# The opening of a hybrid decoder block: the first norm's modulation on VectorE and TensorE instead of GpSimd

## The chip, the cores and the metric

The kernel runs on one core of a Trainium2 chip. The metric is the device time of one execution in microseconds, taken as the median of several runs. A core has five engines that run side by side and meet through semaphores: TensorE (PE in the profile), VectorE (DVE), ScalarE (ACT), GpSimd (POOL) and SyncE (SP), which issues all the transfers (DMAs) of this kernel. Each engine works through its own queue strictly in order.

## The reference

One block on 1024 tokens of width 1024 in float32. A conditioning vector `c` gives six vectors for shift, scale and gate; the first two modulate the first norm:

```python
mod = jax.nn.silu(c) @ w_ada[l] + b_ada[l]
sh1, sc1, g1, sh2, sc2, g2 = jnp.split(mod, 6, axis=-1)
h = modulate(rms_norm(x, norm1_g[l]), sh1, sc1)      # h * (1 + sc1) + sh1
x = x + g1[:, None, :] * token_mixer(h, w_in[l], ...)
h = modulate(rms_norm(x, norm2_g[l]), sh2, sc2)
x = x + g2[:, None, :] * squared_relu_mlp(h, w_ff1[l], w_ff2[l])
return rms_norm(x, norm_f_g)
```

`rms_norm` multiplies by `rsqrt(mean(x*x) + 1e-6)` of each token. The token mixer has a retention branch of four heads and a dilated attention branch of twelve, with a relative bias that is looked up from a table of 32 buckets; both start from `h @ w_in`.

## The kernel before, in words

Everything is kept transposed: a tile `xt[k]` holds 128 of the 1024 channels on its partitions and all 1024 tokens along the free axis (`k` = 0 to 7). A product of full precision is made of three: every operand is split into a high part (`hh`, `raw_..h`, rounded by ACT) and a low part (`hl`, `raw_..l`, the remainder, by DVE), and `mm3` issues low x high, high x low and high x high. A column block of a projection is thus 8 x 3 products for each half of the tokens.

The change touches the opening, which ends where the regular steps begin.

- `startup` loads `c`, the bias table, the eight `xt` tiles, constants (`ct`, `vec`), the first three weight tiles (`raw`) and the columns of `w_ada` for the scale and the shift of the first norm, sixteen tiles of 512 KB called `em` (`early_mod`, nine buffers). The order in which these loads are issued is written out by hand; SP's queue keeps it.
- `cb` is silu(c), spread over all partitions. One element of the scale or shift vector per partition is the sum over the free axis of `em * cb` (`mod1_mul`, `mod1_sum`). For the six tiles `i = SC1 + k` with `k` = 0, 1, 2, 4, 6 and the first shift tile, DVE does product and sum in one instruction (line 328). For the other ten GpSimd multiplies (line 330) and ACT sums (line 338).
- ACT squares the `xt` tiles, DVE adds them into `acc1`; `rstd_rows` sums over the partitions by eight products with a column of ones (in two chains, one for each half of the tokens), DVE scales, GpSimd raises to the power -0.5; `rstd_bcast` spreads the result over the partitions by products with the identity, and ACT copies it to `rb1`.
- `bias_row` looks up one row of the relative bias for each of twelve heads by a product that writes the same row to all 128 partitions; ACT copies it (`rows`), and at the end of the opening SP stores each of the twelve to DRAM (line 635), where the attention reads it much later.
- `h1_scale(k)` adds the bias of the shift (line 357), makes the factor (line 358), scales `xt[k]` by factor and `rb1` (line 361) and lets ACT add the shift and round it to `hh[k]` (line 362). `h1_low(k)` forms `hl[k]` on DVE (line 365).
- `step_first` runs three column blocks at once, `q0`, `q1` and `k0` (two halves `k0a`, `k0b`), tile by tile as `h` becomes ready; the blocks of the last tiles follow in one piece. Its queue order on each engine is the order of the calls in the loop. `step_third` rotates the results; then comes `qkp`, the second block of the keys, and `v`, with four tiles of `w_rv`.

Weight tiles come through a ring of three buffers (`Steps.run`): a tile is loaded when the one three before it has been split.

Of the kernel before, what the change touches and what calls it, by code (L numbers as in the profile page):

```python
# [10 lines left out]
F32 = mybir.dt.float32  # L11
# [116 lines left out]
def block_kernel(ctx, tc, io, stop=None, dbg=None):  # L128
# [3 lines left out]
    def fv(t):  # L132
        return t.bitcast(F32)
# [77 lines left out]
    spool = st_ctx.enter_context(tc.tile_pool(name="spool", bufs=1))  # L211
    xt = [spool.tile([P, S], F32, name=f"xt{k}") for k in range(NK)]
    rb1 = spool.tile([P, S], F32, name="rb1")
    bias_d = [[dram.tile([P, 384], F32, name=f"biasd{g}_{a}") for a in range(4)] for g in range(3)]
    early = []

    def early_mod():

        i = len(early)
        if i < 16:  # L220
            t = spool.tile([P, 1024], F32, tag="em", bufs=9, name=f"em{i}")
            nc.sync.dma_start(t, io["w_ada"][(SC1, SH1)[i % 2] + i // 2])
            early.append(t)

# [14 lines left out]
    def rstd_bcast(rs, b0, nb, name):  # L239
# [4 lines left out]
                             ident, start=True, stop=True)  # L244
        return rb[:, :nb * P]

    bs1 = spool.tile([P, NK], F32, name="bs1")
    rel = spool.tile([P, 12], F32, name="rel")
    onehot = spool.tile([P, 3 * 384], F32, name="onehot")
    rows = spool.tile([P, 12, 384], F32, name="rows")  # L250
    crow = spool.tile([P, S], F32, tag="sq", bufs=2, name="crow")[:1]
    orow = spool.tile([P, S], F32, tag="sq", bufs=2, name="orow")[:1, :P]
    acc1 = spool.tile([P, S], F32, name="acc1")
    first = {}

    def startup(issue, prepare, n_gate, n_loads):
        first["release"] = lambda: issue(n_gate)
        first["release all"] = lambda: issue(n_loads)
        nc.vector.memset(rel, 0.0)
        nc.vector.memset(rel[32:33], 1.0)  # L260
        nc.vector.memset(orow, 1.0)
        nc.gpsimd.memset(onehot, 0.0)
# [11 lines left out]
        issue(2)  # L274
        early_mod()
        early_mod()
        issue(3)
        for _ in range(5):
            early_mod()
        pc = ps_mm("pc")  # L280
        for j in range(2):
            nc.tensor.matmul(pc[:, j, :], orow, crow[:, j * 512:(j + 1) * 512], start=True, stop=True)
        nc.scalar.activation(cb, pc.rearrange("p a b -> p (a b)"), AF.Silu)
        for k in range(NK):
            for j in ((slice(0, S),) if k < NK - 1 else (slice(0, 512), slice(512, S))):
                if k == 0:
                    nc.scalar.activation(acc1, xt[k], AF.Square)
                else:
                    sq = spool.tile([P, S], F32, tag="sq", bufs=2, name=f"sq{k}")
                    nc.scalar.activation(sq[:, j], xt[k][:, j], AF.Square)  # L290
                    nc.vector.tensor_add(acc1[:, j], acc1[:, j], sq[:, j])
            copies, products = (((), ()), ((), ()), ((), (0, 1, 2)), ((0,), (3,)), ((1, 2), (4, 5)),
                                ((3, 4), (6, 7)), ((5, 6), (8,)), ((7, 8), (9,)))[k]
            for i in copies:
                bias_copy(i)
            for i in products:
                bias_row(i)
        rs = [rstd_rows(acc1[:, j * 512:(j + 1) * 512], f"n1{j}", spool) for j in range(2)]
        bias_copy(9)
        prepare(1)  # L300
        mod1(0)
        nc.vector.tensor_scalar_add(bs1, vec[:, VC_BADA + SC1:VC_BADA + SC1 + NK], 1.0)
        prepare(1)
        mod1_mul(1)
        for j in range(2):
            nc.scalar.copy(rb1[:, j * 512:(j + 1) * 512], rstd_bcast(rs[j], 0, 4, f"n1{j}"))
        for i in (10, 11):
            bias_row(i)
        h1_scale(0)
        first["low"]()  # L310
        h1_low(0)
        mod1_sum(1)

    def bias_row(i):

        first[i] = ps_s(f"pb{i}")
        nc.tensor.matmul(first[i][:, :384], rel[:, i:i + 1].to_broadcast([P, P]),
                         onehot[:, (i // 4) * 384:(i // 4 + 1) * 384], start=True, stop=True)

    def bias_copy(i):  # L320
        nc.scalar.copy(rows[:, i, :], first.pop(i)[:, :384])

    def mod1_mul(k):

        for i in (SC1 + k, SH1 + k) if k < NK else ():
            t = early[2 * k + (i < SC1)]
            if k == 0 or i >= SC1 and k not in (3, 5, 7):
                nc.vector.scalar_tensor_tensor(t, t, 1.0, cb, op0=ALU.mult, op1=ALU.mult, accum_out=mods[:, i:i + 1])
            else:
                nc.gpsimd.tensor_mul(t, t, cb)  # L330
                first["sum", k] = first.get(("sum", k), []) + [(t, i)]

    def mod1_sum(k, n=2):

        while n > 0 and first.get(("sum", k)):
            n -= 1
            t, i = first["sum", k].pop(0)
            nc.scalar.activation(t, t, AF.Identity, accum_out=mods[:, i:i + 1])

    def mod1(k):  # L340
        mod1_mul(k)
        mod1_sum(k)

    def mod_prep(i):

# [6 lines left out]
    def mod_load(i):  # L352
        return io["w_ada"][i], mod_prep(i)

    def h1_scale(k):
        sh = mods[:, SH1 + k:SH1 + k + 1]
        nc.vector.tensor_add(sh, sh, vec[:, VC_BADA + SH1 + k:VC_BADA + SH1 + k + 1])
        nc.vector.scalar_tensor_tensor(a1[:, k:k + 1], mods[:, SC1 + k:SC1 + k + 1], bs1[:, k:k + 1],
                                       vec[:, VC_N1 + k:VC_N1 + k + 1], op0=ALU.add, op1=ALU.mult)
        t = xt[k]  # L360
        nc.vector.scalar_tensor_tensor(t, t, a1[:, k:k + 1], rb1, op0=ALU.mult, op1=ALU.mult)
        nc.scalar.activation(hh[k], t, AF.Identity, bias=sh)

    def h1_low(k):
        nc.vector.scalar_tensor_tensor(hl[k], xt[k], mods[:, SH1 + k:SH1 + k + 1], fv(hh[k]),
# [227 lines left out]
    def wsplit(ap):  # L593
        return ap, split_w

    def step_first(ahead, w0, w1):

        ps0, ps1 = ps_mm("q0"), ps_mm("q1")
        ps2 = [ps_s("k0a"), ps_s("k0b")]
        for k in range(NK):  # L600
            early_mod()
            early_mod()
            if k == 0:
                ahead()
                h1_scale(1)
                first["low"]()
                h1_low(1)
                mod1(2)
                bias_copy(10)
                bias_copy(11)  # L610
            if k + 2 < NK:
                if k == 0:
                    mod1_mul(3)
                    mod1_sum(3, 1)
                    h1_scale(2)
                    mod1_sum(3)
                    h1_low(2)
                    mod1(4)
                    h1_scale(3)
                else:  # L620
                    mod1(k + 4)
                    if k + 3 < NK:
                        h1_scale(k + 3)
                    h1_low(k + 2)
            if k < NK - 2:
                proj_mm(ps0, w0, [k])
                proj_mm(ps1, w1, [k])
            if 0 < k < 5:
# [12 lines left out]
    def early_split(raw):  # L641
        hi = whl.tile([P, 1024], F32R, tag="wh", name=raw.name + "h")
        lo = whl.tile([P, 1024], F32R, tag="wl", name=raw.name + "l")
        nc.scalar.copy(hi, raw)
        first["w"] = hi, lo
        first["low"] = lambda: nc.vector.tensor_sub(lo, raw, fv(hi))
        return hi, lo

    early_split.weight = True
# [6 lines left out]
        for j, ps in enumerate(first["ps"][2]):  # L656
            rot1(0, 1, ps, slice(512 * j, 512 * j + 512))

    steps.add(step_first, [wsplit(io["w_rq"][0]), (io["w_rq"][1], early_split)], manual=True)
    steps.add(step_third, [(io["w_rk"][0], early_split)])  # L660

    def qk_step(h, which, i):
# [1049 lines left out]
def pack(x, c, w_ada, b_ada, norm1_g, w_in, rel_bias, ret_gn_g, ret_gn_b,  # L1712
# [45 lines left out]
```

## Time and profile before

| | us |
|---|---|
| median of three runs | 2400.97 (2400.75 to 2401.01) |
| the profiled execution | 2401.76 |
| its span, first to last instruction | 2400.0 |
| PE busy | 2326.6 |
| first projection product (`q`) starts | 36.31 |
| last `hl` ends | 75.22 |
| first `qkp` product starts | 88.53 |

The tables below name an engine, a line of the kernel, an operation and its tiles as `out<-in`; x is a count. PEld is the weight load of TensorE, which overlaps its products. In a stretch of the span the engines' busy times follow one another (PE, PEld, DVE, ACT, POOL), then the granted TensorE clock as a share of full speed, the busy share of the DMA engines and GB/s. A wait is given as total, number and longest, in us. A line of the timeline begins with the start and the length in us; lines of several instructions are merged.

### The profile page before, as it was taken

To read this page: it belongs to the slowest core of one execution; us is meant where nothing else is said; L and a number is where in the kernel's file an instruction comes from. 1 tells how busy PE (TensorE), PEld (TensorE's weight loads), DVE (VectorE), ACT (ScalarE), POOL (GpSimd) and SP (SyncE) were. 2 spreads that over 40 slices of the span, in tenths; PEclk is the share of its full clock that TensorE was granted. 3 is DMA by queue.
4 is the path that set the end of the run, shared out by engine and by line. 5 is a ranking of instruction groups with operands and counts; after the bars stand their busy time and mean duration, and the time that the engine had idled before them with its cause. 6 is when DMAs were issued, how large, how long until landed. Compare 5 with 4: busy or idle time off the path is not lost.

```text
span 2400.0 us, 26494 instructions
## 1 busy us (share of the span) xinstructions
PE 2326.6 (97%) x10716; PEld 1921.9 (80%) x10716; DVE 1199.1 (50%) x1656; ACT 762.5 (32%) x1367; POOL 263.6 (11%) x164
## 2 busy tenths in 40 slices
PE   5999999999999999999998999999899999999998
PEld 3788888888888888878877888887678887888887
DVE  7656137326614743344344135665765554544445
ACT  4333124213411333443253121123354444211212
POOL 5112011201101110000000004501100000000003
PEclk8999999999999999999999999999999999999999
DMA  7312212311321221131131332334123334433222
GB/s 279 111 53 93 84 62 80 127 66 53 114 79 44 88 99 44 46 108 53 45 90 47 111 107 96 96 117 173 45 106 114 108 115 165 157 94 99 89 96 71
DMA packets 87961, 229.49 MB, mean 96 GB/s; under 512 B 20860, under 2 KB 32252, under 8 KB 87710
## 3 DMA queue, kind: packets, MB, share of 16 engines
q1 hardware_dynamic: 87838, 227.79, 28.6%
q8 instruction: 84, 1.38, 0.2%
q14 instruction: 39, 0.32, 0.0%
HBM read 181.26 MB, written 46.50 MB: 95 GB/s over the span
## 4 chain that ended last, share of the span: by engine, by line
PE 87%; DVE 6%; ACT 2%; DMA 2%; issue 1%; SPq 0%; POOLq 0%; POOL 0%; DVEq 0%; ACTq 0%
PE f L183 8%; PE f L187 8%; PE f L185 8%; PE ro L185 2%; PE rg L185 2%; PE rg L183 2%; PE ro L183 2%; PE ro L187 2%; PE rg L187 2%; PE v L493 2%; PE v L494 2%; PE v L492 2%; PE qkp L185 2%; PE qkp L183 2%; PE qkp L187 2%; PE av L494 2%
## 5 line engine op out<-in xcount | busy, mean ns | idle before, releaser
L1555 DVE SCALAR_TENSOR_TENSOR x1r<-f,mods,x1r 128x512 f32<-128x512 f32 x112 | 78.7, 746 | 153.8 <-PE f L187 153.8
L1215 POOL TENSOR_TENSOR g<-g,rt 128x1024 f32<-128x1024 f32 x24 | 66.3, 2764 | 647.7 <-DMA raw<-u 585.1
L1257 POOL TENSOR_TENSOR accnf<-accnf,sqnf 128x256 f32<-128x256 f32 (+1 forms) x18 | 16.6, 924 | 659.0 <-ACT sqnf L1256 659.0
L508 DVE TENSOR_TENSOR vl<-v,vh 128x512 fp32r<-128x512 f32 x32 | 22.1, 690 | 122.2 <-ACT vh L507 122.2
L452 POOL TENSOR_TENSOR j<-qk,j 128x512 fp32r<-128x512 f32 x32 | 43.1, 1346 | 320.6 <-ACT j L451 320.6
L430 DVE TENSOR_TENSOR qk<-qkp,cossin 128x1024 f32<-128x1024 f32 x6 | 7.3, 1218 | 137.3 <-PE qkp L187 137.3
L1214 DVE TENSOR_TENSOR rt<-ro,g 128x1024 f32<-128x1024 f32 x32 | 39.0, 1219 | 57.4 <-PE ro L187 57.4
L507 ACT CAST vh<-v 128x512 fp32r<-128x512 f32 x32 | 18.8, 588 | 149.9 <-PE v L494 149.9
L1390 ACT ACTIVATE a<-a 128x512 f32<-128x512 f32 x48 | 30.4, 632 | 110.0 <-DVE a L1389 110.0
L834 DVE TENSOR_TENSOR P<-sc,bias 128x512 f32<-128x512 f32 x32 | 22.2, 692 | 75.5 <-PE sc L187 74.1
L857 ACT ACTIVATE P<-P,ng 128x128 f32<-128x128 f32 (+1 forms) x96 | 41.9, 438 | 51.5 <-DVE ng L854 51.5
L1363 DVE TENSOR_TENSOR wc<-w1r,wc 128x512 fp32r<-128x512 f32 x48 | 34.2, 719 | 38.7 <-ACT wc L1362 38.7
L183 PE MATMUL f<-h2h,wc 128*128 128x512 f32 x128 | 51.4, 401 | 0.4 <-ACT u L1400 0.4
L187 PE MATMUL f<-h2h,wc 128*128 128x512 f32 x128 | 51.0, 398 | 0.0
L185 PE MATMUL f<-h2l,wc 128*128 128x512 f32 x128 | 50.9, 397 | 0.0
L695 ACT COPY av<-av 128x512 f32<-128x512 f32 x24 | 14.1, 589 | 106.4 <-PE av L494 106.4
L438 POOL TENSOR_TENSOR qk<-qk,t 128x1024 f32<-128x1024 f32 x8 | 19.2, 2400 | 247.0 <-DVE t L436 247.0
L472 ACT COPY sm<-sT 128x128 f32<-128x128 f32 x32 | 8.5, 267 | 114.8 <-PE sT L463 111.4
L347 DVE SCALAR_TENSOR_TENSOR raw<-raw,cb 128x1024 f32<-128x1024 f32 x32 | 44.2, 1380 | 0.0
L1391 ACT ACTIVATE a<-a 128x512 f32<-128x512 f32 x64 | 40.5, 632 | 2.0
L522 ACT COPY on<-oT 128x128 f32<-128x128 f32 x128 | 24.6, 279 | 40.9 <-PE oT L520 40.9
L569 DVE TENSOR_TENSOR statel<-state,stateh 128x512 fp32r<-128x512 f32 x56 | 36.2, 689 | 1.5 <-ACT stateh L568 0.9
(3504 smaller groups left out, 7111.1 us busy)
## 6 DMA issues: line engine op xcount, KB each, us to landing
raw<-in_w_ada_dram SPq DMA_DIRECT2D x32, 512.0 KB, 3.7
w1r<-in_w_ff_dram SPq DMA_DIRECT2D x32, 512.0 KB, 4.9
ad<-a SPq DMA_DIRECT2D x32, 512.0 KB, 3.0
raw<-in_w_ff_dram SPq DMA_DIRECT2D x32, 512.0 KB, 3.6
raw<-ad SPq DMA_DIRECT2D x32, 512.0 KB, 4.4
em<-in_w_ada_dram SPq DMA_DIRECT2D x16, 512.0 KB, 8.4
raw<-in_w_rv_dram SPq DMA_DIRECT2D x16, 512.0 KB, 3.6
raw<-in_w_rg_dram SPq DMA_DIRECT2D x16, 512.0 KB, 3.9
```

Of the source, the lines that this page charges most:

```text
L183: nc.tensor.matmul(o, wl, xh, start=first, stop=False, skip_group_check=skip)
L185: nc.tensor.matmul(o, wh, xl, start=False, stop=False, skip_group_check=skip)
L187: nc.tensor.matmul(o, wh, xh, start=False, stop=last, skip_group_check=skip)
L347: nc.vector.scalar_tensor_tensor(raw, raw, 1.0, cb, op0=ALU.mult, op1=ALU.mult, accum_out=mods[:, i:i + 1])
L452: nc.gpsimd.tensor_sub(t[:, 1], src, fv(t[:, 0]))
L492: nc.tensor.matmul(ps, hl[k][:, tok], w[0][:, ws], start=k == 0, stop=False)
L493: nc.tensor.matmul(ps, hh[k][:, tok], w[1][:, ws], start=False, stop=False)
L494: nc.tensor.matmul(ps, hh[k][:, tok], w[0][:, ws], start=False, stop=k == NK - 1)
L857: nc.scalar.activation(v, v, AF.Exp, bias=ng[:, blk:blk + 1], accum_out=st[:, g, blk, 2 + a:3 + a])
L1215: (nc.vector if h == H - 1 else nc.gpsimd).tensor_add(m, m, t)
L1391: nc.scalar.activation(o, o, AF.Square)
L1555: nc.vector.scalar_tensor_tensor(x, ps[hf], mods[:, G2 + i:G2 + i + 1], x, op0=ALU.mult, op1=ALU.add)
```

## The change

The modulation sums of the first norm leave GpSimd and ACT. Twelve of the sixteen `em` tiles are done by DVE in one instruction each (`mod1_dve`). The first four tiles of the shift (`k` < `NPE` = 4) are packed on the host by columns instead of rows, and TensorE sums them: eight products with a column of `ccol`, which is silu(c) with the channels on the partitions (`mod1_pe`). `em` has twelve buffers. The twelve heads' bias rows are looked up by three products (one for each group of heads, twelve rows each), copied by three ACT copies, stored to a small DRAM tile and spread to the twelve destinations by DRAM to DRAM copies (`bias_out`). The rstd of all 1024 tokens goes through one chain. `h1_scale` is split: `h1_mods(k)` makes the shift (from PSUM for `k` < 4) and the factor, `h1_scale(k)` does the rest. The first tile is scaled in two halves straight from PSUM; `rb1` is copied later. The loads of `ct` and `vec` move between the `xt` tiles. In `step_first` the first tile's products run in another order for `q0`, and tile `k + 1` is prepared in iteration `k`.

```diff
+    brow_d = [dram.tile([12, 384], F32, name=f"browd{g}") for g in range(3)]
@@ early_mod
-            t = spool.tile([P, 1024], F32, tag="em", bufs=9, name=f"em{i}")
+            t = spool.tile([P, 1024], F32, tag="em", bufs=12, name=f"em{i}")
@@ startup
+        nc.sync.dma_start(ccol, io["ccol"])
         for k in range(NK):
             nc.sync.dma_start(xt[k], io["xT"][k])
             if k == 2:
-                nc.sync.dma_start(onehot[:33], io["onehot"])
-        nc.sync.dma_start(ct, io["cst"])
-        issue(1)
-        early_mod()
-        early_mod()
-        nc.sync.dma_start(vec, io["vec"])
...
+                nc.sync.dma_start(onehot[:33], io["onehot"].rearrange("p (g y) -> p g y", g=3))
+            if k == 4:
+                nc.sync.dma_start(ct, io["cst"])
+                nc.sync.dma_start(vec, io["vec"])
+        for i in range(3):
+            early_mod()
+            early_mod()
+            issue(i + 1)
+        for _ in range(6):
             early_mod()
...
+        nc.scalar.activation(ccol, ccol, AF.Silu)
...
-        rs = [rstd_rows(acc1[:, j * 512:(j + 1) * 512], f"n1{j}", spool) for j in range(2)]
-        bias_copy(9)
-        prepare(1)
-        mod1(0)
+            if 2 < k < 6:
+                bias_rows(k - 3)
+        mod1_dve(SC1)
+        rs = rstd_rows(acc1, "n1", spool)
+        mod1_pe(0)
         nc.vector.tensor_scalar_add(bs1, vec[:, VC_BADA + SC1:VC_BADA + SC1 + NK], 1.0)
         prepare(1)
-        mod1_mul(1)
+        h1_mods(0)
+        first["rb"] = [rstd_bcast(rs, 4 * j, 4, f"n1{j}") for j in range(2)]
+        mod1_pe(1)
         for j in range(2):
-            nc.scalar.copy(rb1[:, j * 512:(j + 1) * 512], rstd_bcast(rs[j], 0, 4, f"n1{j}"))
-        for i in (10, 11):
-            bias_row(i)
-        h1_scale(0)
-        first["low"]()
+            h1_scale(0, j)
+        first["lows"].pop(0)()
+        mod1_dve(SC1 + 1)
         h1_low(0)
-        mod1_sum(1)
+        prepare(1)
+
+    def bias_rows(g):
+
+        ps = ps_s(f"pb{g}")[:12, :384]
+        nc.tensor.matmul(ps, rel[:33], onehot[:33, g], start=True, stop=True)
+        nc.scalar.copy(rows[:12, g], ps)
+
+    def bias_out():
+
+        for g in range(3):
+            nc.sync.dma_start(brow_d[g], rows[:12, g])
+        for g in range(3):
+            for a in range(4):
+                nc.sync.dma_start(bias_d[g][a], brow_d[g][4 * g + a:4 * g + a + 1].to_broadcast([P, 384]))
+
+    def mod1_dve(i):
+
+        t = early[2 * (i % 8) + (i < SC1)]
+        nc.vector.scalar_tensor_tensor(t, t, 1.0, cb, op0=ALU.mult, op1=ALU.mult, accum_out=mods[:, i:i + 1])
+
+    def mod1_pe(k):
+
+        ps = first["m", k] = ps_s(f"m{k}")
+        for j in range(NK):
+            nc.tensor.matmul(ps[:, :1], early[2 * k + 1][:, j * P:j * P + P], ccol[:, j:j + 1],
+                             start=j == 0, stop=j == NK - 1)
@@ h1_scale
+    def h1_scale(k, j=None):
+
+        ts = slice(0, S) if j is None else slice(512 * j, 512 * j + 512)
+        t = xt[k][:, ts]
+        nc.vector.scalar_tensor_tensor(t, t, a1[:, k:k + 1], rb1 if j is None else first["rb"][j],
+                                       op0=ALU.mult, op1=ALU.mult)
+        nc.scalar.activation(hh[k][:, ts], t, AF.Identity, bias=mods[:, SH1 + k:SH1 + k + 1])
@@ step_first
+        for j, rb in enumerate(first["rb"]):
+            nc.scalar.copy(rb1[:, 512 * j:512 * j + 512], rb)
         for k in range(NK):
             early_mod()
             early_mod()
...
+            if k < 2:
+                first["lows"].pop(0)()
+            if k + 1 < NK:
+                h1_mods(k + 1)
+                h1_scale(k + 1)
+                if k == 0:
+                    ahead(1)
+                if k + 2 < NK:
+                    mod1_dve(SC1 + k + 2)
+                    if k + 2 >= NPE:
+                        mod1_dve(SH1 + k + 2)
+                h1_low(k + 1)
             if k == 0:
...
+                (wh, wl), (xh, xl) = w0, (hh[0], hl[0])
+                for n, (w, x) in enumerate(((wh, xh), (wh, xl), (wl, xh))):
+                    for j in range(2):
+                        nc.tensor.matmul(ps0[:, j, :], w[:, :P], x[:, 512 * j:512 * j + 512], start=n == 0, stop=False)
+            elif k < NK - 2:
+                proj_mm(ps0, w0, [k])
             if k < NK - 2:
-                proj_mm(ps0, w0, [k])
                 proj_mm(ps1, w1, [k])
+            if k + 2 < NPE:
+                mod1_pe(k + 2)
...
-        for i in range(12):
-            nc.sync.dma_start(bias_d[i // 4][i % 4], rows[:, i, :])
+        bias_out()
@@ pack
-        "w_ada": np.ascontiguousarray(A(w_ada)[0].T).reshape(48, P, D),
+        "ccol": np.ascontiguousarray(_vec(A(c)[0])),
+        "w_ada": np.concatenate([_cols(A(w_ada)[0][:, :4 * P]),
+                                 np.ascontiguousarray(A(w_ada)[0][:, 4 * P:].T).reshape(44, P, D)]),
```

More of the change, by code (lines that the diff above doesn't have):

```diff
@@ L245, in rstd_bcast @@
         return rb[:, :nb * P]
+    NPE = 4
     bs1 = spool.tile([P, NK], F32, name="bs1")
     rel = spool.tile([P, 12], F32, name="rel")
-    onehot = spool.tile([P, 3 * 384], F32, name="onehot")
-    rows = spool.tile([P, 12, 384], F32, name="rows")
+    onehot = spool.tile([P, 3, 384], F32, name="onehot")
+    rows = spool.tile([P, 3, 384], F32, name="rows")
     crow = spool.tile([P, S], F32, tag="sq", bufs=2, name="crow")[:1]
     orow = spool.tile([P, S], F32, tag="sq", bufs=2, name="orow")[:1, :P]
+    ccol = spool.tile([P, NK], F32, name="ccol")
     acc1 = spool.tile([P, S], F32, name="acc1")
@@ L307, in startup @@
-        for i in (10, 11):
-            bias_row(i)
-        h1_scale(0)
-        first["low"]()
-        h1_low(0)
-        mod1_sum(1)
[L314 to L342, printed above, removed]
+            h1_scale(0, j)
+        first["lows"].pop(0)()
+        mod1_dve(SC1 + 1)
+        h1_low(0)
+        prepare(1)
[3 more added lines that the diff above has]
+        nc.scalar.copy(rows[:12, g], ps)
@@ L353, in mod_load, with h1_mods @@
         return io["w_ada"][i], mod_prep(i)
-    def h1_scale(k):
+    def h1_mods(k):
         sh = mods[:, SH1 + k:SH1 + k + 1]
-        nc.vector.tensor_add(sh, sh, vec[:, VC_BADA + SH1 + k:VC_BADA + SH1 + k + 1])
+        nc.vector.tensor_add(sh, first.pop(("m", k))[:, :1] if ("m", k) in first else sh,
+                             vec[:, VC_BADA + SH1 + k:VC_BADA + SH1 + k + 1])
         nc.vector.scalar_tensor_tensor(a1[:, k:k + 1], mods[:, SC1 + k:SC1 + k + 1], bs1[:, k:k + 1],
                                        vec[:, VC_N1 + k:VC_N1 + k + 1], op0=ALU.add, op1=ALU.mult)
-        t = xt[k]
-        nc.vector.scalar_tensor_tensor(t, t, a1[:, k:k + 1], rb1, op0=ALU.mult, op1=ALU.mult)
-        nc.scalar.activation(hh[k], t, AF.Identity, bias=sh)
+    def h1_scale(k, j=None):
[4 more added lines that the diff above has]
+        nc.scalar.activation(hh[k][:, ts], t, AF.Identity, bias=mods[:, SH1 + k:SH1 + k + 1])
     def h1_low(k):
@@ L602, in step_first @@
             early_mod()
-            if k == 0:
[L604 to L624, printed above, removed]
+            if k < 2:
[10 more added lines that the diff above has]
+                h1_low(k + 1)
+            if k == 0:
+                (wh, wl), (xh, xl) = w0, (hh[0], hl[0])
[4 more added lines that the diff above has]
+                proj_mm(ps0, w0, [k])
             if k < NK - 2:
-                proj_mm(ps0, w0, [k])
                 proj_mm(ps1, w1, [k])
+            if k + 2 < NPE:
+                mod1_pe(k + 2)
+            if k == 1:
+                ps2 += [ps_s("k0a"), ps_s("k0b")]
             if 0 < k < 5:
@@ L645, in early_split @@
         first["w"] = hi, lo
-        first["low"] = lambda: nc.vector.tensor_sub(lo, raw, fv(hi))
+        first.setdefault("lows", []).append(lambda: nc.vector.tensor_sub(lo, raw, fv(hi)))
         return hi, lo
@@ L657, in step_third @@
             rot1(0, 1, ps, slice(512 * j, 512 * j + 512))
-    steps.add(step_first, [wsplit(io["w_rq"][0]), (io["w_rq"][1], early_split)], manual=True)
+    steps.add(step_first, [(io["w_rq"][0], early_split), (io["w_rq"][1], early_split)], manual=True)
     steps.add(step_third, [(io["w_rk"][0], early_split)])
```

14 lines of the change are left out of this document (1 added, 13 removed).

## The prediction

> **What bounds the kernel now.** I read the page's engine shares first, then the answer by stretches of the span, TensorE's waits in the opening, and the timeline of the opening.
>
> ```profile
> PE 2326.6 (97%) x10716; PEld 1921.9 (80%) x10716; DVE 1199.1 (50%) x1656; ACT 762.5 (32%) x1367; POOL 263.6 (11%) x164
> ...
> 18.00:36.30 18.30, 6.99 (x36) 5.57 (x36) 16.93 (x16) 5.56 (x10) 14.69 (x7) 0.70 0.86 352
> 36.30:64.67 28.37, 17.90 (x51) 11.76 (x51) 26.93 (x23) 11.88 (x19) 15.81 (x6) 0.74 0.62 217
> 64.67:88.30 23.63, 23.63 (x93) 19.32 (x94) 16.17 (x20) 12.01 (x16) 1.88 (x1) 0.89 0.20 74
> 99.20:200.00 100.80, 100.80 (x477) 84.16 (x476) 59.31 (x113) 29.57 (x74) 18.29 (x15) 1.00 0.20 63
> ...
> PE q L183 <- ACT hh L362: 13.0, 3, 9.9
> PE q L185 <- DVE hl L365: 7.4, 4, 4.2
> ```
>
> PE is the bound of the whole. From 64.67 to 200 us it has no idle time, so whatever brings the end of `step_first` forward (the first `qkp` product starts at 88.53) brings the end of the program forward by as much. In 18 to 64.67 us DVE is the busy one (43.9 of 46.7 us) and PE waits for `hh` and `hl`, 20.4 us in all. The timeline shows why DVE is slow there:
>
> ```profile
> 22.49 2.08 PE L243 MATMUL n11rb<-ct,n11rs 128*128 128x128 f32 x8 [0.65 <-POOL n11rs L236]
> 27.06 16.82 POOL L330 TENSOR_TENSOR em<-em,cb 128x1024 f32<-128x1024 f32 x6 [1.01 <-DMA em<-in_w_ada_dram]
> 27.14 2.28 DVE L357 TENSOR_TENSOR mods<-mods,vec 128x1 f32<-128x1 f32 x1
> 31.81 3.26 DVE L361 SCALAR_TENSOR_TENSOR xt<-xt,a,rb 128x1024 f32<-128x1024 f32 x1
> 35.00 3.38 DVE L646 TENSOR_TENSOR raw_223l<-raw,raw_223h 128x1024 fp32r<-128x1024 f32 x1
> 38.30 3.36 DVE L365 SCALAR_TENSOR_TENSOR hl<-xt,mods,hh 128x1024 fp32r<-128x1024 f32 x1
> ...
> 62.13 1.28 DVE L361 SCALAR_TENSOR_TENSOR xt<-xt,a,rb 128x1024 f32<-128x1024 f32 x1
> 63.34 1.28 DVE L365 SCALAR_TENSOR_TENSOR hl<-xt,mods,hh 128x1024 fp32r<-128x1024 f32 x1
> 64.53 1.22 DVE L328 SCALAR_TENSOR_TENSOR em<-em,cb 128x1024 f32<-128x1024 f32 x1
> ```
>
> While GpSimd multiplies `em` tiles, many a DVE instruction takes some 2 us more: 3.26 against 1.28 for the same scaling, 2.28 against 0.15 for a one-column add. Ten instructions show it, 21 us together against their undisturbed rows.
>
> **The change part by part.** Times are those of the profiled execution (2401.76 us, span 2400.0), 0.79 above the median of 2400.97.
>
> *Sum of squares.* Seven copies of bias rows (0.42 each) stand in ACT's queue ahead of the last square; three will. But DVE's adds set the pace: four in 5.22 us, and DVE waited only 0.17 and 0.48 us afterwards, so at most 0.65 us is there to gain. Against it stand a Silu of eight columns on ACT (about 0.2), one more load on SP's queue (0.36), and `ct` and `vec` moved ahead of three `xt` tiles (0.13 MB; at the 0.41 MB/us the loads run at, 0.3). I take nothing: 18.8 us for the last add, with ends of -0.65 and +0.9.
>
> *One chain for the rstd, and `mod1_pe(0)`.* PE's ten bias products (8.62 us) become three, issued together, so PE stands idle from about 13 to 18.2 us. After idle stretches of 2.4 and 2.7 us (before 54.90 and 63.13) the granted clock was 0.5, so I cost what follows at half clock. The eight one-column `n1ss` products are 16 passes; four such products at half clock (`n21ss`, at 1709 us) start 0.21 us apart per pass: 3.4 us, to 21.6. (At full clock, `n10ss`, 0.117 per pass: 1.9 us.) The square root of eight columns on GpSimd (1.02 for four; 1.84 in the other row, beside DVE) is covered: PE meanwhile runs `mod1_pe(0)`, eight products of the same form, to 25.0. Behind it in PE's queue stand the two broadcasts, 1.9 us each at half clock (the row of `n11rb`), to 28.8. DVE scales the second half of `xt0` from PSUM in 0.7 (512 columns from PSUM: 0.69) and is free at 29.6; in the kernel before it finished that scaling at 35.07. The one new wait on DVE, the shift's bias add behind `mod1_pe(0)`, ends at 25; behind it stands only this scaling, which waits for the broadcasts anyway. Gain so far 35.07 - 29.6 = 5.4 us. At full clock it would be free at 26.4: that end is kept. `mod1_pe(1)` then fills PE to 32, before its first projection (36.31 before); `hl0` is only due at 33, so this costs nothing.
>
> *The rest on DVE.* The order after 29.6 us has 11 modulation products, 7 scalings, 8 `hl`, 3 weight remainders and 7 pairs of one-column steps. With GpSimd's products gone I take the spacings of the undisturbed stretch 62 to 69 us: 1.15, 1.21, 1.19, 1.19 and 0.32. That is 12.65 + 8.47 + 9.52 + 3.57 + 2.24 = 36.45, and 1.35 for two `hl` that wait for ACT's `hh` (1.15 each, the last quite uncovered): 37.8. The last `hl` ends at 67.4, against 75.22. So DVE takes over six products (6.9 us), and still needs 37.8 us where it took 40.15: 2.35 gained. ACT loses ten sums (12.3 us) and is nowhere late. Twelve `em` buffers in place of nine let the loads run through: 14.4 MB at 0.41 MB/us, the last tile landing near 40 us (from the known landings: `raw_223` at 20.84, 6.58 MB), and DVE needs it at 58. Free.
>
> *PE after the last `hl`.* 40 products of 512 columns remain (4 of `q0`, 12 of `q1`, 24 of `k0`), 0.227 each: 9.1. DVE delivers a tile every 5.0 us, PE needs 4.1 for k = 2 to 4 and then only 2.7 and 1.4, so it idles some 2 us twice before the last tile and will be at half clock again. In 64.67 to 69.5 us twelve products ran at 0.427: 2.4 us lost, which I add. End at 67.4 + 9.1 + 2.4 = 78.9, against 88.53; the third term is 13.3 - 11.5 = 1.8. `mod1_pe(2)` and `(3)` (1.9 to 3.4 each) lie in PE's slack at k = 0 and 1.
> The clock gate is also described in the Trainium skill (TensorE: Matmul & The Clock Gate, "What's actually happening"): half rate until a window of about 3.4 us has been busy. By that the lost time would be 8 products, an estimate of 1.6 us, and the end 78.1; this trace's half-clock run lasted 4.8 us.
>
> *Bias rows out.* SP issues three small stores and twelve copies from DRAM to DRAM in place of twelve stores (11.82 us of issue before). They stand behind `cossin` and `decay` (landing near 47) and ahead of the third `w_rv` tile, which cannot issue before its buffer is free: the remainder of `w_rk`'s second tile, near 68. The twelve stores moved 2.36 MB at some 396 GB/s; copies at a quarter of that still end near 74, and the tile is needed 13 us later than it could be used (issued 82.91, usable 88.7, used by the fifth k of `v` at 101.9). Hidden; bounds 0 and a few us.
>
> Sum: 5.4 + 2.35 + 1.8 = 9.6 us. 2401.76 - 9.6 = 2392.2 profiled, 2391.4 as a median (span 2390.4).
>
> **Rivals.**
> (a) *The small products do not cost half clock*, because they count as PE work and the clock rises while they run. DVE is then free at 26.4, the last `hl` ends at 64.2: 3.2 us more, and up to 2.4 more if the tail stays warm: 2386 to 2389. For it: PE is busy without a break from 18.2 on. Against it: before, `n10ss`, `n11ss` and `n10rb` ran from 18.28 to 21.84 and `n11rb` was then at clock 0.5. By the rule on that page of the Trainium skill, that one busy window lifts the clock, this rival would hold.
> (b) *The opening is later*: the adds end up to 0.9 late behind `ct` and `vec`, the square root takes 1.84 and is not covered, and DVE's tile takes 5.4 us rather than 5.0. End at 81 to 84, 2393.5 to 2397.
> (c) *Slower: PE stays at half clock through `step_first`*, since DVE now feeds it in pieces. From 32 us, 144 x 0.427 + 6.8 = 68.3, to 100.3: 2413. It decides at 85 half-clock products (32.6 + 6.8 + 0.2 x 85 = 56.4 us); the run before had about 33. Against it: at half clock a tile's 18 products take 7.7 us, more than DVE's 5.0, so PE would catch no idle time and warm up, as it did three times before.
> (d) *The gain does not reach the end*: the third `w_rv` tile is stuck behind the copies. PE stalls in `v` if that tile issues after 86.5 (101.9 - 9.6 less 5.8 from issue to use), so if the twelve, starting near 49, take over 37 us; at 47 us all is lost: 2401.
>
> **How the numbers follow.** Forecast 0.53 (2389.5 to 2393.5), (a) 0.19, (b) 0.18, (c) 0.05, (d) 0.05. The range 2386.5 to 2397 holds the first three but the edges of (a) and (b). A measurement tells 0.2% (4.8 us) from no change; the forecast, (a) and most of (b) lie beyond that: faster 0.87, within 0.2% 0.07, slower 0.06.
>
> **What would show it.** Right: no DVE instruction over 1.4 us in 25 to 75 us; `n1ss` and the first `mod1_pe` at 0.2 us per pass; first projection near 32, last `hl` near 67, first `qkp` near 79; no PE wait from there to 200 us. Wrong: `em` products waiting for loads, PE at clock 0.5 beyond 45 us outside the last tiles, or a PE wait for `w_rv`'s third tile in `v`.

## The result and the profile after

The changed kernel takes 2390.61 us in the median of six runs (2389.77 to 2395.58), beside 2400.99 for the kernel before on the same chip: a ratio of 0.9961 with a 95% interval of 0.9948 to 0.9974. Its executions fall into two groups, four near 2390.5 and two near 2395; the profile came from one of the latter (2395.58), so a second profile of the same kernel, from an execution of 2391.92 us, is read beside it, and the prediction is held against that one.

The shares of the page and the stretches of the span, for the changed kernel in the execution of 2395.58 us:

```profile
PE 2336.5 (98%) x10762; PEld 1933.8 (81%) x10762; DVE 1184.5 (49%) x1667; ACT 748.6 (31%) x1340; POOL 233.4 (10%) x152
...
18.00:36.30 18.30, 16.25 (x74) 15.15 (x75) 10.53 (x19) 4.90 (x7) 1.64 (x1) 0.90 1.03 409
36.30:64.67 28.37, 27.64 (x117) 22.79 (x116) 23.54 (x38) 6.19 (x7) 0.00 (x0) 0.83 0.71 233
64.67:88.30 23.63, 20.34 (x74) 15.20 (x73) 16.71 (x21) 6.30 (x6) 4.76 (x2) 0.86 0.09 23
88.30:200.00 111.70, 111.70 (x525) 93.13 (x525) 65.84 (x123) 32.86 (x77) 19.81 (x16) 1.00 0.23 71
```

GpSimd (the fifth pair of numbers in a stretch) is empty from 36.30 to 64.67, where it had 15.81 us before. PE's idle time there has shrunk from 10.5 to 0.7 us, but PE is now idle for 3.3 us behind 64.67, where it had none. The timeline of PE in the opening, same execution:

```profile
18.19 3.57 PE L232 MATMUL n1ss<-ct,acc 128*128 128x1 f32 x16 [4.62 <-DVE acc L292]
21.62 3.55 PE L333 MATMUL m<-ccol,em 128*128 128x1 f32 x16
25.04 2.05 PE L244 MATMUL n10rb<-ct,n1rs 128*128 128x128 f32 x8
26.88 1.91 PE L244 MATMUL n11rb<-ct,n1rs 128*128 128x128 f32 x8
```

The four groups lie within 0.1 us of where the prediction put them. The two executions of this one kernel part behind 34 us. First the stretches 34 to 38, 38 to 42 and 42 to 46 us of the execution of 2395.58 us, then the same of the one of 2391.92 us:

```profile
34.00:38.00 4.00, 4.00 (x12) 3.14 (x12) 3.84 (x7) 2.08 (x2) 0.00 (x0) 0.50 1.04 413
38.00:42.00 4.00, 4.00 (x17) 3.81 (x18) 2.37 (x5) 0.00 (x0) 0.00 (x0) 0.50 1.01 400
42.00:46.00 4.00, 4.00 (x11) 3.12 (x10) 3.02 (x4) 1.15 (x1) 0.00 (x0) 0.50 1.04 418
```

```profile
34.00:38.00 4.00, 4.00 (x20) 3.34 (x19) 3.83 (x7) 2.09 (x2) 0.00 (x0) 0.74 1.04 413
38.00:42.00 4.00, 4.00 (x25) 3.51 (x25) 3.96 (x7) 1.04 (x1) 0.00 (x0) 1.00 1.02 404
42.00:46.00 4.00, 4.00 (x25) 3.52 (x25) 3.89 (x7) 1.13 (x2) 0.00 (x0) 1.00 1.03 414
```

In the slower one the granted clock (third number from the end) stays at 0.50 until 46 us, in the other it is full again from 38 to 66. (Both fell to half rate at 33.1 us, after PE had waited 1.8 us for the first `hl`.) DVE's waits in 18 to 90 us tell what this costs; the longest of the slower execution, then of the faster:

```profile
DVE mods L349 <- PE m L333: 7.7, 3, 3.2
```

```profile
DVE mods L349 <- PE m L333: 3.2, 1, 3.2
```

The wait of 3.2 us is the foreseen one, for `mod1_pe(0)`. The other two (1.6 and 2.9 us) are for `mod1_pe(2)` and `mod1_pe(3)`, which stand in PE's queue behind products that run at half clock; in the faster execution they don't exist. So the last `hl` ends at 72.1 there and at 67.5 here, and the first `qkp` product starts at 83.58 and 79.59 (88.53 before). The end of that opening in the execution of 2391.92 us, by the timelines of DVE and PE:

```profile
29.50 1.22 DVE L646 TENSOR_TENSOR raw_224l<-raw,raw_224h 128x1024 fp32r<-128x1024 f32 x1
...
66.18 1.28 DVE L363 SCALAR_TENSOR_TENSOR hl<-xt,mods,hh 128x1024 fp32r<-128x1024 f32 x1 [1.22 <-ACT hh L360]
```

```profile
66.20 0.76 PE L183 MATMUL q<-hh,raw_224l 128*128 128x512 f32 x2 [1.50 <-ACT hh L360]
67.52 1.22 PE L185 MATMUL q<-hl,raw_224h 128*128 128x512 f32 x2 [0.56 <-DVE hl L363]
68.54 1.05 PE L187 MATMUL q<-hh,raw_224h 128*128 128x512 f32 x2
...
79.59 0.62 PE L183 MATMUL qkp<-hh,raw_500l 128*128 128x512 f32 x2
```

From 29.50 to its last `hl` DVE is never held back for longer than the 1.22 us for ACT's last `hh`; PE loses its clock just before the last tile (pairs of products 0.85 us apart from 67.52 to 73.65, against 0.46 at full clock).

### The profile page after: what moved, and what is told of

It reads as the page before. It is cut to its first block, busy times and chain, and to the rows that moved or that the text cites. A ratio compares the mean times of both kernels' runs of the same rounds, so it can differ in the third digit from the quotient of the medians.

```text
span 2393.8 us, 26558 instructions
## 1 busy us (share of the span) xinstructions
PE 2336.5 (98%) x10762; PEld 1933.8 (81%) x10762; DVE 1184.5 (49%) x1667; ACT 748.6 (31%) x1340; POOL 233.4 (10%) x152
## 4 chain that ended last, share of the span: by engine, by line
PE 88%; DVE 5%; DMA 3%; ACT 2%; issue 1%; SPq 0%; POOLq 0%; POOL 0%; DVEq 0%; ACTq 0%
PE f L187 8%; PE f L185 8%; PE f L183 8%; PE rg L183 2%; PE rg L185 2%; PE ro L185 2%; PE ro L183 2%; PE v L490 2%; PE ro L187 2%; PE rg L187 2%; PE v L492 2%; PE v L491 2%; PE gate L183 2%; PE gate L185 2%; PE gate L187 2%; PE qkp L183 2%
## 5 line engine op out<-in xcount | busy, mean ns | idle before, releaser
L428 DVE TENSOR_TENSOR qk<-qkp,cossin 128x1024 f32<-128x1024 f32 x6 | 7.3, 1217 | 137.2 <-PE qkp L187 137.2
L505 ACT CAST vh<-v 128x512 fp32r<-128x512 f32 x32 | 18.8, 587 | 150.4 <-PE v L492 150.4
```

## The experiments

The theory: GpSimd's ten products made the DVE instructions beside them some 2 us longer, and to be rid of them is the whole gain; the sums on PE, the fewer bias rows and the single chain only shift where things wait. The main rival: the gain comes from the new opening (one chain, sums on PE), and the sixteen products would be too much for DVE. Further questions are what the one-column products at half rate cost, and what is lost at the tail.

| kernel | median, us | lowest to highest | ratio to before (95%) | first `qkp` starts | last `hl` ends |
|---|---|---|---|---|---|
| changed kernel | 2390.61 | 2389.77 to 2395.58 | 0.9961 (0.9948 to 0.9974) | 83.6 (79.6) | 72.1 (67.5) |
| all products on DVE alone | 2390.62 | 2386.66 to 2390.77 | 0.9945 (0.9928 to 0.9961) | 75.8 | 66.5 |
| the same, three bias products | 2389.36 | 2386.46 to 2389.91 | 0.9951 (0.9937 to 0.9966) | 76.3 | 67.0 |
| all products on DVE, other tail | 2388.61 | 2387.87 to 2391.22 | 0.9942 (0.9921 to 0.9963) | 77.3 | 67.1 |
| changed, no sums on PE | 2392.82 | 2391.03 to 2394.16 | 0.9959 (0.9944 to 0.9974) | 80.4 | 70.0 |
| changed, GpSimd busy | 2408.72 | 2406.57 to 2409.18 | 1.0034 (1.0021 to 1.0047) | 97.4 | 86.5 |
| changed, later sums earlier | 2390.62 | 2388.29 to 2390.91 | 0.9948 (0.9933 to 0.9963) | 77.9 | 67.7 |
| changed, PE kept busy | 2387.18 | 2385.99 to 2387.51 | 0.9935 (0.9920 to 0.9950) | 75.9 | 65.0 |
| changed, other tail | 2387.16 | 2382.96 to 2388.20 | 0.9941 (0.9927 to 0.9956) | 74.2 | 68.1 |
| the last three together | 2381.14 | 2378.77 to 2384.94 | 0.9920 (0.9903 to 0.9936) | 73.2 | 67.1 |
| the same, more idle products | 2384.18 | 2383.91 to 2384.59 | 0.9921 (0.9905 to 0.9938) | 71.6 | 65.5 |

The last two columns are of the profiled execution; the numbers in brackets are of the second profile of the changed kernel. The runs were spread over several chips, whose medians of the kernel before lie between 2400.99 and 2402.32 us; each ratio is to the kernel before on the same chip, so where two rows are close the ratio is the better measure.

**One part alone: all sixteen products on DVE.** The kernel before, with one condition changed; two chains, twelve bias rows and order stay.

```diff
-            if k == 0 or i >= SC1 and k not in (3, 5, 7):
+            if True:
```

> The kernel before with one thing changed: all sixteen modulation products of the first norm on VectorE, none on GpSimd and none of the sums on ScalarE; bias rows, rstd chains and load order as before. Theory A (the gain is GpSimd off VectorE's back): ten more VectorE products cost 11.5 us, ten slowed instructions give back 21 us; no VectorE instruction over 1.4 us in the opening, last hl near 66 us, 2391 to 2393. Theory B (the gain comes from the bias rows, the single rstd chain and TensorE's share of the sums): at most 3 us faster, 2398 or more.

Measured: 2390.62 us, the time of the whole change. The groups of DVE in 18 to 80 us, of the kernel before and then of this one (line, engine, operation, tiles, count, then busy us and mean ns):

```profile
L365 DVE SCALAR_TENSOR_TENSOR hl<-xt,mods,hh 128x1024 fp32r<-128x1024 f32 x8 | 14.1, 1761 | 1.3 <-ACT hh L362 1.2
L361 DVE SCALAR_TENSOR_TENSOR xt<-xt,a,rb 128x1024 f32<-128x1024 f32 x8 | 12.3, 1532 | 0.4
```

```profile
L328 DVE SCALAR_TENSOR_TENSOR em<-em,cb 128x1024 f32<-128x1024 f32 x16 | 18.8, 1217 | 0.0
L361 DVE SCALAR_TENSOR_TENSOR xt<-xt,a,rb 128x1024 f32<-128x1024 f32 x8 | 10.3, 1284 | 0.4
L365 DVE SCALAR_TENSOR_TENSOR hl<-xt,mods,hh 128x1024 fp32r<-128x1024 f32 x8 | 10.2, 1280 | 1.4 <-ACT hh L362 1.2
```

DVE takes ten more products and is still done with the last `hl` at 66.5 us (75.22 before), because everything else on it runs at its undisturbed length. The first scaling, too, ends at 28.48 (27.20 + 1.28) with the two old chains, a microsecond before the changed kernel's 29.5. So the 5.4 us that the prediction booked under the one chain were GpSimd's doing as well.

**The cause on its own: GpSimd busy again.** In the changed kernel GpSimd does ten products that nothing needs.

```diff
         mod1_pe(1)
+        for _ in range(10):
+            nc.gpsimd.tensor_mul(acc1, acc1, cb)
```

> The changed kernel with ten products of 128 x 1024 put on GpSimd from 23 us on, whose result is not used and for which nothing waits in the opening. Theory A (GpSimd's products slow VectorE's instructions beside them): VectorE instructions of 2 to 3.5 us return between 24 and 52 us, some ten of them at 2 us each, last hl 10 to 20 us later than in the changed kernel, 2400 to 2412. Rival (VectorE was slow before for another reason, the loads running at full rate or the waits for the sums): no VectorE instruction over 1.4 us, 2390 to 2395.

Measured: 2408.72 us, slower than before the change (by 0.21 to 0.47%), and 18.1 us above the changed kernel. DVE's timeline while these products run (to 53.4 us):

```profile
27.43 0.75 DVE L360 SCALAR_TENSOR_TENSOR xt<-xt,a,n10rb 128x512 f32<-128x512 f32 x1 [1.11 <-PE n10rb L244]
29.14 0.75 DVE L360 SCALAR_TENSOR_TENSOR xt<-xt,a,n11rb 128x512 f32<-128x512 f32 x1 [0.96 <-PE n11rb L244]
29.80 2.45 DVE L648 TENSOR_TENSOR raw_224l<-raw,raw_224h 128x1024 fp32r<-128x1024 f32 x1
...
35.46 3.35 DVE L365 SCALAR_TENSOR_TENSOR hl<-xt,mods,hh 128x1024 fp32r<-128x1024 f32 x1
38.73 3.39 DVE L648 TENSOR_TENSOR raw_230l<-raw,raw_230h 128x1024 fp32r<-128x1024 f32 x1
42.04 0.14 DVE L351 TENSOR_TENSOR mods<-m,vec 128x1 f32<-128x1 f32 x1
42.11 2.26 DVE L353 SCALAR_TENSOR_TENSOR a<-mods,bs,vec 128x1 f32<-128x1 f32 x1
```

The instructions with both inputs in SBUF take 3.35 us in place of 1.2 to 1.3, a one-column one 2.26 in place of 0.21. Those that read PSUM beside it (the halves of `xt`, `mods` from `m`) keep their 0.75 and 0.14. This is the rule of the Trainium skill (SBUF — State Buffer, "Who interferes with whom"): a DVE instruction with two SBUF inputs contends with a GpSimd instruction that reads SBUF, one with at most one such input, outside the 2-port modes, doesn't. The trace agrees on both halves. (A row of the kernel before lies outside the plain pair: `bs<-vec`, with one SBUF input, took 2.30 us beside a GpSimd product, and 0.16 in the changed kernel; no run shows which mode it ran in.) The trace adds what each engine pays. Four of the ten GpSimd products, three of them ahead of 31.2 us, took 2.35 us each; the other six, beside DVE's large products, took 3.20 to 3.24. So each such DVE product loses some 2.1 us and each such GpSimd product some 0.9: the two take turns, one GpSimd product and one DVE product in about 3.3 us. The kernel before shows the same (2.34 and 3.34). GpSimd's share costs nothing here, because nothing waits for these products.

**Does it matter how few bias rows there are?** The first experiment with the change's three bias products, copies and DRAM tile as well.

```diff
+            if 2 < k < 6:
+                bias_rows(k - 3)
...
-        for i in range(12):
-            nc.sync.dma_start(bias_d[i // 4][i % 4], rows[:, i, :])
+        bias_out()
```

> The kernel before with all products on VectorE (the first experiment) and, besides, the bias rows in three products with their copies from DRAM to DRAM. Theory A (the seven products fewer only let TensorE cool down before the partition sums): those sums and broadcasts at half clock, VectorE free for the second tile 2 to 4 us later than in the first experiment, 2391 to 2395. Rival (fewer copies on ScalarE bring the opening forward): 2386 to 2390.

Measured: 2389.36 us, not to be told from 2390.62 (the ratios are 0.9951 and 0.9945). The norm's first products start earlier (17.80 against 18.94) and run at half rate, since PE has stood idle ahead of them (timeline of PE, this kernel):

```profile
17.80 1.87 PE L232 MATMUL n10ss<-ct,acc 128*128 128x1 f32 x8 [4.84 <-DVE acc L292]
```

1.87 us in place of 1.05: what the shorter queue gains, the clock takes back, and the scaling starts at 27.68 in place of 27.20. That is theory A's mechanism at a quarter of its price or less: 0.5 us, where 2 to 4 were expected, and the time came out in the rival's range.

**Does it matter that PE sums four tiles?** The changed kernel with `NPE = 0`: all sixteen tiles by rows, their sums on DVE.

```diff
-    NPE = 4
+    NPE = 0
...
-        mod1_pe(0)
+        mod1_dve(SH1)
...
```

> The changed kernel with no sum on TensorE: the four shift tiles go to VectorE too and are packed by rows again. Theory A (TensorE's small products hold VectorE up, because they run at half clock in front of the rstd broadcasts and behind the first tiles' projections): VectorE pays 4 x 1.15 = 4.6 us, but its three waits for these sums (7.7 us in the profile) go, and the broadcasts come 3.5 us earlier; not slower than the changed kernel, 2387 to 2391. Rival (TensorE's share is a real part of the gain): 2394 to 2396, some 4.6 us slower than the changed kernel's faster executions.

Measured: 2392.82 us; neither side of the expectation is met cleanly, and the ratio (0.9959) doesn't part it from the changed kernel (0.9961). Without the sums PE should have been free for the broadcasts 3.5 us earlier, and wasn't (timelines, this kernel):

```profile
21.70 1.22 DVE L327 SCALAR_TENSOR_TENSOR em<-em,cb 128x1024 f32<-128x1024 f32 x1
21.86 2.55 POOL L237 TENSOR_TENSOR n1rs<-n1rs,ct 128x8 f32<-128x8 f32 x1 [21.42 <-DVE n1rs L236]
24.47 2.07 PE L244 MATMUL n10rb<-ct,n1rs 128*128 128x128 f32 x8 [2.89 <-POOL n1rs L237]
```

GpSimd's one small instruction, 1.64 us in the changed kernel, takes 2.55 beside a DVE product, and PE waits 2.89 us for it. So to drop the sums brings the broadcasts only 0.6 us forward (24.47 against 25.04). The sums spare DVE four products (4.9 us by the mean of 1217 ns); the medians differ by 2.2 us, the ratios by nothing.

**The later sums earlier.** `mod1_pe(2)` and `(3)` each one tile ahead, so that the projections don't stand before them.

```diff
         mod1_pe(1)
+        mod1_pe(2)
...
-            if k + 2 < NPE:
-                mod1_pe(k + 2)
+            if k + 3 < NPE:
+                mod1_pe(k + 3)
```

> The changed kernel with the sums of shift tiles 2 and 3 issued one projection tile earlier on TensorE (tile 2 before the first projection, tile 3 before the second). Theory A: VectorE's waits of 1.6 and 2.9 us for these sums go, last hl near 67.5 instead of 72.1 in the profiled execution, first qkp near 79, 2387 to 2390, and the executions no longer split into 2390.5 and 2395. Rival (VectorE is held by something else there): unchanged, 2390 to 2395 with the split.

Measured: 2390.62 us, the median of the changed kernel to 0.01. Of the waits for `m` only the first (3.2 us) is left, and none of its four runs is above 2391. This is what the second profile says too: those two waits are no part of the usual execution. That the slower group is gone for good is not shown by four runs.

**What the half rate costs in the opening.** Four idle products of 512 columns behind the bias rows, whose result nothing reads, keep PE at work until the norm's first product.

```diff
+            if k == 5:
+                fill = ps_mm("fill")
+                for n in range(4):
+                    nc.tensor.matmul(fill[:, n % 2, :], xt[0][:, :P], xt[1][:, :512], start=True, stop=True)
```

> The changed kernel with four idle products of 512 columns on TensorE between the bias products and the partition sums (13.5 to 18 us; their result is not used). Theory A (the small products cost 0.21 us per pass because TensorE has cooled down by then): n1ss at 0.117 us per pass, VectorE free for the second tile 2 to 3 us earlier, 2387.5 to 2392. Rival (one-column products run at that rate in any case, or lower the clock themselves at once): nothing gained, 2390 to 2396.

Measured: 2387.18 us (2385.99 to 2387.51), below every run of the changed kernel, though the intervals of the two ratios still touch (to 0.9950, from 0.9948). The timeline of PE:

```profile
19.13 1.84 PE L232 MATMUL n1ss<-ct,acc 128*128 128x1 f32 x16
20.83 1.93 PE L337 MATMUL m<-ccol,em 128*128 128x1 f32 x16
...
25.45 3.41 PE L337 MATMUL m<-ccol,em 128*128 128x1 f32 x16
```

The same sixteen passes take 1.84 and 1.93 us in place of 3.57 and 3.55, and the first scaling starts at 24.14 in place of 27.13. But the clock is not held: PE works without a longer break than 0.2 us from 19.13 on, and from 24 us the passes are slow again. The record agrees: 0.54 in 24 to 26 us and 0.50 from 26 to 34. Here these small products did not keep the clock up.

**The tail.** In the changed kernel PE waits for the last tiles and then has 40 products left. Here tile 6 of `q0` and `q1` and tiles 4 and 5 of `k0` go into the loop.

```diff
-            elif k < NK - 2:
+            elif k < NK - 1:
                 proj_mm(ps0, w0, [k])
-            if k < NK - 2:
+            if k < NK - 1:
                 proj_mm(ps1, w1, [k])
...
-            if 0 < k < 5:
+            if 0 < k < 7:
                 proj_mm(ps2, first["w"], [k - 1])
...
-        proj_mm(ps0, w0, [6, 7])
-        proj_mm(ps1, w1, [6, 7])
-        proj_mm(ps2, first["w"], [4, 5, 6, 7])
+        proj_mm(ps0, w0, [7])
+        proj_mm(ps1, w1, [7])
+        proj_mm(ps2, first["w"], [6, 7])
```

> The changed kernel with the products of q1 for tile 6 and of k0 for tiles 4 and 5 moved ahead, into the idle time of TensorE before the last tile; 22 products of 512 columns then stand behind the last hl in place of 40. Theory A (the end is the last hl, plus what stands behind it, plus the half clock that the idle time brings): 18 x 0.227 = 4.1 us earlier and 1 to 2.5 us less at half clock, 2385 to 2388 where the changed kernel takes 2390.5. Rival (the end is set by the split of the next weight tile or by the rotation, not by TensorE's backlog): at most 2 us faster.

Measured: 2387.16 us, with a ratio whose interval still overlaps that of the changed kernel. The timelines of DVE and PE:

```profile
66.77 1.28 DVE L363 SCALAR_TENSOR_TENSOR hl<-xt,mods,hh 128x1024 fp32r<-128x1024 f32 x1 [1.22 <-ACT hh L360]
...
74.17 0.70 PE L183 MATMUL qkp<-hh,raw_500l 128*128 128x512 f32 x2 [0.72 <-DVE qk L429]
```

The first `qkp` starts 6.1 us after the last `hl`, where the changed kernel takes 12.1; PE waits for `hl` 1.2 us in all, 0.6 at the longest, and never falls to half clock at the end. What holds `qkp` last is now the rotation on DVE (0.72 us), as the rival has it, but for the last bit only. Up to the tail the profiled execution is like the second profile of the changed kernel (half rate until 37 us, against 36; last `hl` at 68.1, against 67.5), so the 5.4 us between 74.2 and 79.6 are the tail's. It is also the fastest of its four by 3.9 us (2382.96), because the rest of the program is shorter as well; the tail doesn't explain that part.

The same edit in the kernel with all products on DVE:

> The kernel before with all products on VectorE and the tail reordered (q0 and q1 of tile 6 and k0 of tiles 4 and 5 in the loop); bias rows, rstd chains and loads as before. Theory A: 4 us earlier than without the reordering, 2384 to 2388. Rival (TensorE is backlogged there, so the order does not matter): 2389 to 2391.

Measured: 2388.61 us with an interval that holds the 2390.62 of the same kernel without it, and the first `qkp` is no earlier (77.3 against 75.8; it now waits 0.72 us for the rotation, which the new order puts off). There the old order of the loop prepares two tiles ahead: PE's last wait for `hl` is over at 62.5 and 63.1 us, ahead of the last two tiles, and what lies behind it is the same work in another order. This points to the change's preparing only one tile ahead as the source of the tail's loss; no run changed that alone.

**All three together**, and once more with the idle products begun earlier (one at `k == 2`, five at `k == 5`):

> The changed kernel with the idle products, the earlier sums and the reordered tail together. Theory A: the gains add, last hl near 64, first qkp near 71 to 72, 2380 to 2384. Rival: the three overlap and it is no faster than the best single one, 2386 to 2388.

> The combination of idle products, earlier sums and reordered tail, with idle products from 8 us on (one ahead of the bias products, five behind them), so that TensorE has been busy for 10 us when the partition sums begin. Theory A (the four idle products of the combination ran at half clock and pushed the sums back to 20.6 us): n1ss starts by 19.3 at 0.117 us per pass, first qkp near 70, 2377 to 2381. Rival (idle products only displace the sums): 2381 or more.

Measured: 2381.14 and 2384.18 us. The first is the fastest kernel here, 0.9920 of the kernel before (0.9903 to 0.9936), an interval that lies wholly below the changed kernel's, but not below those of the single edits. Its time is theory A's, its opening isn't: the last `hl` ends at 67.1 and the first `qkp` starts at 73.2, where 64 and 71 to 72 were expected. Its idle products themselves ran at half rate in the profiled execution (6.61 us for the four; 5.38 in the experiment with them alone) and delayed the norm's first product to 20.55, so that DVE is free for the second tile at 29.10, 0.4 us earlier than in the changed kernel, where the idle products alone gave 26.36. The second misses theory A (the norm's first product at 20.03, 2384.18 us) and meets the rival; by the ratios the two kernels are the same (0.9920 and 0.9921). To begin earlier did bring the opening forward (first `qkp` 71.6 against 73.2), but not the end: the rest of the program, span less that start, took 2311.2 us in place of 2307.7. That rest varies by several us between kernels with the same instructions there (2310.2 and 2310.5 in the two profiles of the changed kernel, 2311.5 before, 2307.0 with the other tail, 2313.1 with DVE alone), and no run here tells why; PE's waits in it that vary most are for ACT's `pth100` and for the second norm.

**The second look** at the changed kernel, used above:

> The changed kernel once more, for a profile of one of its faster executions. Theory A (its executions differ by when TensorE's clock rises behind the first projections, and so by VectorE's wait for the sums of shift tiles 2 and 3): if it is one of the 2390.5 us executions, the first two projection tiles are at full clock at some point between 34 and 44 us, and the waits of 1.6 and 2.9 us are gone or halved. Rival (the difference lies in the rest of the program): the same opening as in the profile, first qkp at 83.6.

Measured: 2391.92 us, with the full clock from 38 to 66 us, no wait for `mod1_pe(2)` or `(3)`, and the first `qkp` at 79.59.

## Why the prediction was right

The time is right: 2391.4 forecast, 2390.61 measured, well inside 2386.5 to 2397. That the two agree to 0.8 us is partly chance, as the sum below shows. By the steps, with the execution of 2391.92 us:

*Sum of squares*: right. The last add ends at 18.7; 18.8 was taken.

*One chain and `mod1_pe(0)`*: right in every time, wrong in the cause. DVE is free at 29.50 (29.6). One ground for the half rate was read a little loosely: after the idle time before 54.90 the products ran at full rate until 56 and only then at half. But "gain so far 5.4 us" stood under the chain; DVE alone with two chains gets there at 28.48. The gain was that the scaling no longer takes 3.26 us and the step before it 2.28; the one chain costs about as much at half rate as its shorter queue saves. The working had both facts and did not put them together: the rows of 2.28 and 3.26 us were shown as those of GpSimd's neighbours.

*The rest on DVE*: right, 37.96 us against 37.8. No DVE instruction there is above 1.3 us, as foretold, and a tile takes 5.0.

*"`mod1_pe(2)` and `(3)` lie in PE's slack at k = 0 and 1"*: holds where the clock rises by 38 us, and fails where it doesn't. That execution also shows a sign that the prediction had named for being wrong, by a hair: PE at clock 0.5 beyond 45 us outside the last tiles (until 46). There, at 2395.58 us, the two sums cost DVE 4.5 us. The price at half rate (3.4) was named; what it would stand behind was not.

*PE after the last `hl`*: 12.1 us against 11.5. The mechanism (idle before the last tile, then half clock) is the one foretold; it was sized too low, since half rate lasts from 67.52 to 73.65, 6.1 us, where 4.8 were taken from the trace before.

*Bias rows out*: right. In the execution of 2395.58 us the first copy issues at 48.55, the last by 56.2 and each lands 5.6 us later (median); the third `w_rv` tile issues at 76.68 (72.01 in the other execution, where near 68 was taken), and PE does not wait from 83.6 to 200 us. (That tile's first use in the kernel before was at 102.13, not 101.9, which changes nothing.)

The three terms come to 5.57 + 2.19 + 1.2 = 9.0, and the start of `qkp` moves by 88.53 - 79.59 = 8.94. The median moved by 10.4, within the scatter of the rest of the program: the third term came out 0.6 smaller than forecast, and the rest of the program more than made up for it. Of the rivals, (a) falls: the small products do run at half rate, 3.57 us where the full rate takes 1.84. The rule that was cited for it, by the Trainium skill (TensorE: Matmul & The Clock Gate, "What's actually happening"), that one busy window of some 3.4 us lifts the clock, does not hold for these as it stands: PE was busy without a break from 18.19 us, and its passes were slow up to 28.6 us, 10.4 us later; only then `mod1_pe(1)` took 2.09. In the kernel with the other tail, whose opening is the same, even that took 3.41 (at 28.73), and the half rate lasted to 37 us. (b) is what the slower executions look like, by another road: at 83.6 us, but from the late sums and not from a late opening. (c) happened for 13 us of one execution and then ended, as the argument against it said. (d) falls.

What the prediction did not see is that the change gives part of its gain away. From 18 to 30 us DVE is busy for 4.3 us, where the kernel with only the products moved is busy for 10.4, because that kernel does four modulation products while the chain runs; and with one tile prepared ahead in place of two, PE runs out of work at the tail. One edited condition gets the same time as the whole change.

## What to carry to other kernels

Where two engines slow each other, look at which instructions are long and which are not before counting the work that is moved: here DVE got faster by taking on all of GpSimd's work, and a small test with useless work on the suspected engine showed the cause at once. When several edits come together, try the plainest alone; and where an engine waits for a short chain, put independent work there, and keep preparing far enough ahead that TensorE does not run dry, and lose its clock, at the end.

## What was not expected of the hardware

- GpSimd and DVE take turns where both read two operands from SBUF, and DVE pays more: DVE's products of 128 x 1024 took 3.35 us in place of 1.28, GpSimd's 3.2 in place of 2.35. GpSimd pays for small instructions too: eight columns took 2.55 us beside a DVE product and 1.64 without one.
- One-column products raised the clock late or not at all, and didn't hold it: in the changed kernel PE needed 10.4 us of them and of small broadcasts before its passes became fast, with the other tail 13.7 us of them did not do it, and in the kernel with idle products the clock fell after 5 us of them.
- The view of the granted clock reads 1.00 from the start of the span to 32 us in the changed kernel, while its passes take what they take at a recorded 0.50 elsewhere (3.41 us at 25.45 in the kernel with idle products). With the other tail it reads 1.00 up to 80 us, while pairs of products start 0.85 us apart until 37. The traces hold no clock record ahead of 29.1 and 37.3 us; up to there the view cannot be trusted here, and the durations can.
- The same kernel raised its clock at some 36 us in one execution and at 46 in another. The two openings, equal to 0.1 us until 34, part by 4 us; what sets the moment stays open.
